# RWKV front and output projection with another ScalarE order, local attention in head pairs: a two-block network on one Trainium2 core

## The chip, the cores and the metric

One core of a Trainium2 chip runs the whole kernel. The metric is the device time of one launch in microseconds (us), taken as the median of several runs. TensorE (PE in the profile) multiplies; VectorE (DVE), ScalarE (ACT) and GpSimd (POOL) do the elementwise work; SyncE (SP) issues most DMAs.

## The reference

Input x has 256 tokens of 1024 channels. Four residual layers follow each other: RWKV-7 time mixing, local attention with sinks, a gated chunk mixer, forgetting attention; each has a feed-forward block behind it. The change touches the first two mixers:

```python
# RWKV-7: xr, xk, xv ... = x + (shifted x - x) * mu[i]
k = xk @ w_rkv[1]
w = -softplus(-(w_decay0 + tanh(xw @ w_decay1) @ w_decay2)) - 0.5
a = sigmoid(a0 + (xa @ a1) @ a2)
kk = heads(k * k_k); k = k * (1 + (a - 1) * k_a)
# S = S*decay + (S a) b^T + v k^T;  y = S r;  y = groupnorm(y)...
h = (y * g) @ w_o
x = x + rms_norm(h, g1);  x = x + conv_ffn(rms_norm(x, g2))
# local attention: 16 query heads on 4 key/value heads, window 128, 2 blocks
s = q k^T * 64**-0.5, masked;  m = max(max(s), sink)
p = exp(s - m);  denom = sum(p) + exp(sink - m)
o = (p / denom) @ v;  h = o @ w_o
```

All is float32. The kernel splits both operands of its large products into a part hi (rounded to the type fp32r that PE takes quickly) and the rest lo, and adds three products, hi*hi + lo*hi + hi*lo.

## The kernel before, in words

**Weights.** Weights of the large products arrive as units of 1 MB (`raw`, 128x2048). `split` makes hi by ScalarE casts (L120, four pieces of 512 columns) and lo by VectorE subtractions (L122). Six lo pieces, two each of units 57 to 59, go to GpSimd instead. A unit's `raw` buffer is refilled by a DMA on SP's queue when its pieces are done. `unit(ahead)` splits so many units ahead of the one handed out.

**Order.** Each engine runs its instructions in the order in which the program issues them; a scheduler sets that order from priorities, and `tc.issue_after(X)` keeps what is issued inside behind X. So a piece of ScalarE work that is ready can stand behind one that is not needed yet, and the reverse.

**RWKV front.** `pw` (L491) is the first low-rank product of decay and gate a; ScalarE turns it into `gw` (L492 tanh, L493 copy). `gw` feeds 32 matmuls `pz` (L512), in four groups m of eight; ScalarE takes the tanh of each (L517, tiles EE and av), VectorE makes the decay out of EE (L518) and runs scans (L530), whose exponentials ScalarE takes (L532, L533). Between them PE forms key blocks `pk` (`k_mm`, L564), of 8 contraction steps (16 records in the trace) each, on two PSUM buffers in turn. ScalarE reads a block by L570 and L571, VectorE by L573 (`kt`), which needs av; only then is its PSUM buffer free for the block after the next. `pn` (L584) are small norm products.

**RWKV output projection (wo).** `down` and `down_tail` multiply the group-normed y (`yT`, made by `gnT`, ScalarE L898 and VectorE L899) with units 16 to 19, tokens t=0 first, then t=1 into `dt`. `mid` runs `gnT(1, .)`. `done` squares the result on ScalarE (`jk_pn`, L175), builds the norm factor (L157 to L162, a short chain between ScalarE and VectorE) and adds the result to x. `nxt['go'](t)` squares the new x (`jk_n`), builds its factor, multiplies (`xn_n`, L227), transposes on PE (`pt_n`, L230) and splits it into X hi (ScalarE L240) and lo (VectorE L241); `nxt['front'](t)` multiplies the first block of the next layer (`F`).

**Local attention.** `swa` walks a list of tokens: `q` and `k` project, `s<n><hg>` forms scores of 128 tokens n and 8 heads hg (PE L1084, VectorE max L1087, ScalarE exponential L1096, VectorE scaling L1105), `p<n><hg>` transposes the probabilities (PE L1118), copies them out of PSUM (L1120) and multiplies with v (L1124, `pos`), `D` multiplies the first unit of the output projection `wo1`. A matmul of L1124 loads 64 columns of v and writes 64 of the 128 output partitions, the lower (e=0) or the upper half (e=1). In local attention the four matmuls of one PSUM buffer go by head; forgetting attention (`pof`) uses the same lines with heads of both halves in turn.

Of the kernel before, what the change touches and what calls it, by code (L numbers as in the profile page):

```python
# [55 lines left out]
def tile_net(ctx: ExitStack, tc: tile.TileContext, x_in, wst, lora1, lora2, cvec, cons, rows, sinks, w_s, foxf, out, dbg=None):  # L56
# [186 lines left out]
    def prep(key, norm=True, fold=False):  # L243
        o = {}

        def go(t):
            if t == 0:
                o['X'] = xhl(xp, f'X_{key}', bufs=1)
            rs = rms_of_x(t, key) if norm else None
            o[t] = rs  # L250
            to_T(t, rs, o['g'], key, *o['X'])
# [15 lines left out]
        o['go'] = go  # L267
        o['front'] = front
# [77 lines left out]
    def down_tail(acc, xs, us, nu, done, nxt):  # L346
        hls = [unit(ahead=len(us) + 2 - i) for i in range(len(us))]
        ga = {'kvg': 12, 'mx0': 12, 'ml1': 9, 'ml0': 9, 'mx1': 9, 'n12': 9, 'n02': 9}.get(nxt['key'] if nxt else '', 99)
        for t in range(2):
            if t and 'mid' in W:  # L350
                W.pop('mid')()
# [4 lines left out]
            for h in range(2):  # L356
# [67 lines left out]
    def rwkv(nxt):  # L424
        with tc.tile_pool(name='rw', bufs=1) as wp:
# [67 lines left out]
            A.copy(gw[64:128], pw[64:128, 0:T])  # L493
# [11 lines left out]
            Ei = EE[:, 32 * 65:].rearrange('p (q x) -> p q x', x=64)  # L505
            for m in range(4):
                pz = [psum(f'pz{m}{wa}', 'acc') for wa in range(2)]
                for f in range(2):
# [4 lines left out]
                for wa in range(2):
                    sg = Ei[:, 8 * m:8 * m + 8, :].rearrange('p c x -> p (c x)') if wa == 0 else av[:, 2 * m:2 * m + 2, :].rearrange('p j t -> p (j t)')
                    for f in range(2):
                        j = wa * 8 + 2 * m + f
                        A.activation(sg[:, f * T:(f + 1) * T], pz[wa][:, f * T:(f + 1) * T], AF.Tanh, bias=hb[:, j:j + 1], scale=0.5)  # L517
# [42 lines left out]
            def k_mm(u, f):  # L560
                w3 = kw[u].rearrange('p (k c) -> p k c', k=KD)
                pk = psum(f'pk{u}_{f}')[:, 0:T]
                for k in range(KD):
                    PE.matmul(pk, lhsT=w3[:, k, f * P:(f + 1) * P], rhs=XK[:, k, :], start=k == 0, stop=k == KD - 1)  # L564
# [5 lines left out]
                A.activation(s1[:, fs], pk, AF.Square, scale=cvc('k_k', j))  # L570
                A.activation(kkr[:, fs], pk, AF.Copy, scale=cvc('k_k', j))  # L571
# [310 lines left out]
            def gnT(t, hf):  # L882
# [15 lines left out]
                A.copy(YH[:, ks, tsl], p4)  # L898
                V.tensor_tensor(out=YL[:, ks, tsl], in0=p4, in1=YH[:, ks, tsl].bitcast(F32), op=ALU.subtract)  # L899
# [155 lines left out]
    def attend(ap, qT, kT, vv, oview, kidx, vidx, Lof, bias, sink, gate, nm, rsq=None):  # L1055
# [7 lines left out]
        def scores(n, hg):  # L1063
# [31 lines left out]
            for i in range(8):  # L1095
                A.activation(L[:, i, 0:nk], L[:, i, 0:nk], AF.Exp, bias=ng[:, i:i + 1], scale=1.0 if rsq is None else rsq[n], accum_out=dn[:, i:i + 1])  # L1096
            if sink is not None:
                sk = ap.tile([P, 8], F32, tag='sk', name=f'sk{nm}{n}{hg}', bufs=2)
                V.tensor_tensor(out=ej(sk), in0=sks, in1=ej(ng), op=ALU.add)
                A.activation(sk, sk, AF.Exp)  # L1100
                V.tensor_tensor(out=dn, in0=dn, in1=sk, op=ALU.add)
# [436 lines left out]
```

## Time and profile before

| what | value |
|---|---|
| median of 3 runs | 1349.07 us (1347.24 to 1349.47) |
| profiled execution, own time | 1347.06 us |
| its span, first to last instruction | 1345.4 us |
| PE busy | 1312.2 us, 98% |
| VectorE, ScalarE, GpSimd busy | 991.3 us (74%), 817.5 us (61%), 76.0 us (6%) |
| mean granted TensorE clock | 0.988 of full speed |
| HBM read | 222.32 MB, 166 GB/s over the span with what is written |

The share of busy time is a mean over the whole program; a PE that is 98% busy has 33 us of idle time in it, which stand at a few places. The list of waits names these places, and the timeline shows which engine worked in them.

### The profile page before, as it was taken

The numbers are of one execution on the slowest core, as the hardware profiler recorded it, in microseconds if no ns is written. First come the engines' busy times: TensorE is split into PE (matmuls) and PEld (weight loads), VectorE is DVE, ScalarE is ACT, GpSimd is POOL, SyncE is SP. The second block draws the span as 40 slices with busy tenths as digits, with TensorE's granted clock in tenths as the row PEclk, the third lists the DMA queues.
The fourth block names the chain that finished last, engine by engine and source line by source line (L and its number), as shares of the span: only waits on it lengthen the run. The fifth ranks groups of instructions, "written<-read, shape, count | busy, mean of one in ns | idle before, by whom it ended". The sixth has DMA issues, their size and how long they took to land.

```text
span 1345.4 us, 20651 instructions
## 1 busy us (share of the span) xinstructions
PE 1312.2 (98%) x7700; PEld 1108.6 (82%) x7700; DVE 991.3 (74%) x2200; ACT 817.5 (61%) x1803; POOL 76.0 (6%) x103
## 2 busy tenths in 40 slices
PE   7999997999999999999999999999999999999998
PEld 5785875888888878888888998888887888888887
DVE  5558676898888758998888976766667887676663
ACT  4505595776677856776777754655546667555551
POOL 4221400000000100000000000000000000000000
PEclk9899898999999999999999999999999999999999
DMA  9220232565544414655536553665543743265550
GB/s 358 71 86 1 96 104 108 199 247 194 202 168 142 154 66 157 235 212 204 192 130 235 188 187 124 234 218 189 188 168 118 280 150 133 98 243 191 189 188 32
DMA packets 34819, 224.70 MB, mean 167 GB/s; under 512 B 3712, under 2 KB 6048, under 8 KB 8736
## 3 DMA queue, kind: packets, MB, share of 16 engines
q1 hardware_dynamic: 32496, 215.18, 44.5%
q0 software_dynamic: 1472, 5.25, 1.1%
q10 hardware_dynamic: 752, 2.97, 0.6%
q8 instruction: 60, 0.98, 0.3%
q14 instruction: 39, 0.32, 0.1%
HBM read 222.32 MB, written 1.06 MB: 166 GB/s over the span
## 4 chain that ended last, share of the span: by engine, by line
PE 77%; DVE 3%; ACT 3%; DMA 1%; issue 1%; ACTq 0%
PE pu L299 10%; PE pm L299 7%; PE pu L297 6%; PE md L146 4%; PE md L147 4%; PE md L148 4%; PE pm L297 4%; PE fd L146 3%; PE fd L147 3%; PE fd L148 3%; PE pu L295 1%; PE gu L148 1%; PE gu L147 1%; PE gu L146 1%; PE go L146 1%; PE go L148 1%
## 5 line engine op out<-in xcount | busy, mean ns | idle before, releaser
L122 DVE TENSOR_TENSOR lo<-raw,hi 128x512 fp32r<-128x512 f32 x650 | 417.0, 687 | 81.0 <-ACT hi L120 79.6
L120 ACT CAST hi<-raw 128x512 fp32r<-128x512 f32 x656 | 365.1, 618 | 131.6 <-PE md L148 52.7
L299 PE MATMUL pu<-X_n_x,hi 128*128 128x512 f32 x560 | 142.1, 393 | 0.0
L299 PEld LDWEIGHTS pu<-X_n_x,hi 128*128 128x128 f32 x560 | 100.1, 189 | 17.5
L299 PE MATMUL pm<-X_ml_x,hi 128*128 128x512 f32 x392 | 99.7, 393 | 0.0
L297 PEld LDWEIGHTS pu<-X_n_x,lo 128*128 128x128 f32 x640 | 87.4, 190 | 6.2
L297 PE MATMUL pu<-X_n_x,lo 128*128 128x256 f32 x640 | 89.7, 283 | 0.0
L299 PEld LDWEIGHTS pm<-X_ml_x,hi 128*128 128x128 f32 x392 | 70.0, 189 | 12.2
L117 DVE SCALAR_TENSOR_TENSOR lo<-raw,cv,hi 128x256 fp32r<-128x256 f32 (+1 forms) x136 | 67.1, 561 | 14.0 <-ACT hi L116 13.8
L116 ACT ACTIVATE hi<-raw,cv 128x256 fp32r<-128x256 f32 (+1 forms) x136 | 65.7, 560 | 14.9 <-DMA raw<-in_wst 10.9
L304 ACT COPY r<-pm 128x256 f32<-128x256 f32 x56 | 20.9, 373 | 73.5 <-PE pm L299 73.5
L305 DVE TENSOR_TENSOR r<-pm,r 128x256 f32<-128x256 f32 x56 | 23.5, 425 | 56.9 <-ACT r L304 56.8
L297 PEld LDWEIGHTS pm<-X_ml_x,lo 128*128 128x128 f32 x448 | 61.2, 190 | 4.3
L297 PE MATMUL pm<-X_ml_x,lo 128*128 128x256 f32 x448 | 62.7, 282 | 0.0
L1012 ACT ACTIVATE ab<-zs,cv 128x256 f32<-128x256 f32 x80 | 47.8, 600 | 16.6 <-DVE zs L305 16.5
L147 PE MATMUL md<-lo,md0h 128*128 128x512 f32 x128 | 49.9, 390 | 0.0
L146 PE MATMUL md<-hi,md0h 128*128 128x512 f32 x128 | 49.8, 389 | 0.0
L146 PE MATMUL md<-hi,md1h 128*128 128x512 f32 x128 | 49.8, 389 | 0.0
L147 PE MATMUL md<-lo,md1h 128*128 128x512 f32 x128 | 49.8, 389 | 0.0
L148 PE MATMUL md<-hi,md0l 128*128 128x512 f32 x128 | 49.8, 389 | 0.0
L148 PE MATMUL md<-hi,md1l 128*128 128x512 f32 x128 | 49.8, 389 | 0.0
L1013 DVE SCALAR_TENSOR_TENSOR ab<-zs,cv,ab 128x255 f32<-128x255 f32 x80 | 38.6, 482 | 10.9 <-ACT ab L1012 9.3
(563 smaller groups left out, 3088.4 us busy)
## 6 DMA issues: line engine op xcount, KB each, us to landing
raw<-in_wst SPq DMA_DIRECT2D x188, 1024.0 KB, 4.9
kw<-in_wst SPq DMA_DIRECT2D x12, 1024.0 KB, 9.8
g_n<-in_rows POOLq DMA_DIRECT2D x6, 512.0 KB, 3.8
ncb<-cd ACTq DMA_DIRECT2D x2, 1024.0 KB, 5.8
l2g<-in_lora SPq DMA_DIRECT2D x1, 1024.0 KB, 14.6
g_ml<-in_rows POOLq DMA_DIRECT2D x2, 512.0 KB, 3.9
out<-x SPq DMA_DIRECT2D x4, 256.0 KB, 2.0
cs<-in_cons SPq DMA_DIRECT2D x1, 513.0 KB, 9.2
```

Of the source, the lines that this page charges most:

```text
L116: A.activation(hi[:, q:q + w], r[:, q:q + w], AF.Copy, scale=g[:, j:j + 1])
L117: V.scalar_tensor_tensor(out=lo[:, q:q + w], in0=r[:, q:q + w], scalar=g[:, j:j + 1], in1=hi[:, q:q + w].bitcast(F32), op0=ALU.mult, op1=A ...
L120: A.copy(hi[:, q:q + SPL], r[:, q:q + SPL])
L122: pe_.tensor_tensor(out=lo[:, q:q + SPL], in0=r[:, q:q + SPL], in1=hi[:, q:q + SPL].bitcast(F32), op=ALU.subtract)
L146: W['mm'].append(PE.matmul(o, lhsT=lh, rhs=rh, start=start, stop=False))
L147: PE.matmul(o, lhsT=lh, rhs=rl, start=False, stop=False)
L148: PE.matmul(o, lhsT=ll, rhs=rh, start=False, stop=stop)
L297: W['mm'].append(PE.matmul(pt[:, 0:T], lhsT=l3[:, k, fs], rhs=X2[:, 0, k, :], start=False, stop=False))
L299: PE.matmul(pt, lhsT=h3[:, k, fs], rhs=X2[:, :, k, :], start=False, stop=k == KD - 1)
L305: V.tensor_tensor(out=out, in0=pt[:, 0:T], in1=out, op=ALU.add)
L1012: A.activation(ab[:, s, :], z, AF.Identity, bias=cw(3, fi), scale=cw(2, fi))
L1013: V.scalar_tensor_tensor(out=ab[:, s, 1:T], in0=z[:, 0:T - 1], scalar=cw(1, fi), in1=ab[:, s, 1:T], op0=ALU.mult, op1=ALU.add)
```

## The change

It does the following:

- Front: ScalarE takes `gw` (L492, L493) ahead of the six reads of `pk` that stood before it; the reads of the fourth and later key blocks stand behind the last tanh issued (`th`); PE forms the fourth key block (2u+f = 3) behind the second group of `pz`.
- wo: `mid` returns the subtractions of `gnT(1, .)`, and units 16 and 17's last splits are issued behind them, so `yT` goes ahead of the casts; a new `rms(0)` issues the squares of x's first tokens as soon as they are there.
- Local attention: scores, exponentials, scaling, transposes and the products with v go in pairs of heads, one of each half (0, 4, 1, 5, ...); the token order puts the first tokens' last heads (`s01`) ahead and their softmax in a step of its own (`e01`); the first unit of wo1 runs t=1 before t=0. In forgetting attention, exponential and scaling go in the order of pairs too.
- GpSimd's six lo pieces go to VectorE.

```diff
             else:
                 for q in range(0, 2048, SPL):
                     A.copy(hi[:, q:q + SPL], r[:, q:q + SPL])
-                    pe_ = G if {57: 12, 58: 12, 59: 12}.get(i, 0) >> q // SPL & 1 else V
-                    pe_.tensor_tensor(out=lo[:, q:q + SPL], in0=r[:, q:q + SPL], in1=hi[:, q:q + SPL].bitcast(F32), op=ALU.subtract)
+                    V.tensor_tensor(out=lo[:, q:q + SPL], in0=r[:, q:q + SPL], in1=hi[:, q:q + SPL].bitcast(F32), op=ALU.subtract)
...
+        def rms(t):
+            if norm:
+                o['rs0'] = rms_of_x(t, key)
...
-            rs = rms_of_x(t, key) if norm else None
+            rs = o.pop('rs0', None) or rms_of_x(t, key) if norm else None
...
     def down_tail(acc, xs, us, nu, done, nxt):
-        hls = [unit(ahead=len(us) + 2 - i) for i in range(len(us))]
+        hls = [unit(ahead=len(us) + 2 * ('mid' not in W) - i) for i in range(len(us))]
...
             if t and 'mid' in W:
-                W.pop('mid')()
+                for an in W.pop('mid')():
+                    late.enter_context(tc.issue_after(an.ins))
+                split(W['u'] + 2)
+                late.close()
...
+            if nxt is not None and t == 0 and ga < 99:
+                with tc.high_priority():
+                    nxt['rms'](0)
...
-            A.copy(gw[64:128], pw[64:128, 0:T])
+            gwi = A.copy(gw[64:128], pw[64:128, 0:T])
...
-                for k in range(KD):
-                    PE.matmul(pk, lhsT=w3[:, k, f * P:(f + 1) * P], rhs=XK[:, k, :], start=k == 0, stop=k == KD - 1)
+                with tc.issue_after(pzm[1].ins) if 2 * u + f == 3 else nullcontext():
+                    for k in range(KD):
+                        PE.matmul(pk, lhsT=w3[:, k, f * P:(f + 1) * P], rhs=XK[:, k, :], start=k == 0, stop=k == KD - 1)
...
-                A.activation(s1[:, fs], pk, AF.Square, scale=cvc('k_k', j))
-                A.activation(kkr[:, fs], pk, AF.Copy, scale=cvc('k_k', j))
+                with tc.issue_after((gwi if j < 3 else th).ins):
+                    A.activation(s1[:, fs], pk, AF.Square, scale=cvc('k_k', j))
+                    A.activation(kkr[:, fs], pk, AF.Copy, scale=cvc('k_k', j))
...
                 with tc.issue_after(W['mm'][-5].ins):
                     for hf in range(2):
-                        gnT(1, hf)
+                        an = gnT(1, hf)
+                return an
...
-                ss_ = [i0 + i if KZ else (i0 + i) // 2 + 4 * (i % 2) for i in range(per)]
+                ss_ = [(i0 + i) // 2 + 4 * (i % 2) for i in range(per)]
...
-                for i, b in [(i, b) for i in range(per) for b in range(n + 1)] if KZ else [(i, b) for b in range(n + 1) for i in range(per)]:
+                for i, b in [(i, b) for b in range(n + 1) for i in range(per)]:
...
-            for tk in 'q0 k0 k1 q1 s10 q2 s00 q3 s11 p10 p00 s01 D p11 p01'.replace('/', ' ').split():
+            TOK = 'q0 k0 k1 q1 s10 q2 s00 q3 s01 p10 e01 p00 s11 D p01 p11'.split()
...
+                elif tk[0] == 'e':
+                    with tc.issue_after(st['ox', 1, 0].ins):
+                        st.pop(('e', int(tk[1]), int(tk[2])))()
...
-                    for t in range(2):
+                    for t in (1, 0):
```

**ScalarE in the RWKV front, before** (EE and av rows of L517 are the tanh of `pz`, L570 and L571 the reads of `pk`):

```order
L570 ACTIVATE AR<-pk_0_347,cv 128x256
...
L571 ACTIVATE kkr_384<-pk_0_375,cv 128x256
L492 ACTIVATE gw<-pw 64x256
L493 COPY gw<-pw 64x256
L570 ACTIVATE AR<-pk_1_389,cv 128x256
L571 ACTIVATE kkr_384<-pk_1_389,cv 128x256
L517 ACTIVATE EE<-pz_240,hb 128x256 x2
L517 ACTIVATE av<-pz_241,hb 128x256 x2
L517 ACTIVATE EE<-pz_252,hb 128x256 x2
L517 ACTIVATE av<-pz_253,hb 128x256 x2
L532 ACTIVATE EE<-AR 128x8x64
```

The same place now:

```order
L503 ACTIVATE gw<-pw 64x256
L504 COPY gw<-pw 64x256
L584 ACTIVATE AR<-pk_0_347,cv 128x256
...
L585 ACTIVATE kkr_384<-pk_0_375,cv 128x256
L529 ACTIVATE EE<-pz_240,hb 128x256 x2
L529 ACTIVATE av<-pz_241,hb 128x256 x2
L529 ACTIVATE EE<-pz_252,hb 128x256 x2
L529 ACTIVATE av<-pz_253,hb 128x256 x2
L544 ACTIVATE EE<-AR 128x8x64
L545 ACTIVATE EE<-AR 128x512
L544 ACTIVATE EE<-AR 128x8x64
L545 ACTIVATE EE<-AR 128x512
L529 ACTIVATE EE<-pz_264,hb 128x256 x2
```

`gw` moved ahead of the six reads, the fourth block's reads (`pk_1_389`) moved away, and four exponentials now stand ahead of the third group's tanh, where one stood.

**ScalarE in the wo tail, before** (`dt` is the second tokens' result, `x_66` the residual of the first tokens):

```order
L890 ACTIVATE ya_1900<-pyt_1891,cv 128x128 x3
L120 CAST hi_1779<-raw_1742 128x512 x4
L120 CAST hi_1789<-raw_1753 128x512 x4
L898 CAST yT<-ya_1900 128x4x128
L175 ACTIVATE jk_pn_1935,ss_pn_1936<-dt_1909 128x512
L175 ACTIVATE jk_n_1967,ss_n_1968<-x_66 128x512
L175 ACTIVATE jk_n_1972,ss_n_1973<-x_66 128x512
L157 ACTIVATE rs_n_1977<-ss_n_1973,bb_n_1970 128x1
L175 ACTIVATE jk_pn_2028,ss_pn_2029<-dt_1910 128x512
```

The same place now:

```order
L904 ACTIVATE ya_1898<-pyt_1889,cv 128x128 x3
L174 ACTIVATE jk_n_1851,ss_n_1852<-x_66 128x512
L174 ACTIVATE jk_n_1856,ss_n_1857<-x_66 128x512
L912 CAST yT<-ya_1898 128x4x128
L156 ACTIVATE rs_n_1861<-ss_n_1857,bb_n_1854 128x1
L120 CAST hi_1907<-raw_1742 128x512 x4
L120 CAST hi_1917<-raw_1753 128x512 x2
L174 ACTIVATE jk_pn_1953,ss_pn_1954<-dt_1927 128x512
L120 CAST hi_1917<-raw_1753 128x512 x2
L174 ACTIVATE jk_pn_2028,ss_pn_2029<-dt_1928 128x512
```

Two squares and the `yT` cast stand ahead of the eight casts, where `yT` stood behind all eight.

**VectorE at the end of wo1, before** (n120 is the norm of the first tokens for the next feed-forward block, pn111 the norm of wo1's result for the second tokens):

```order
L162 SCALAR_TENSOR_TENSOR rsq_n120_4937<-rv_n120_4938,ry_n120_4940 128x1
L227 SCALAR_TENSOR_TENSOR xn_n1200_4947<-x0_66,rsq_n120_4937,g_n12_4787 128x512
L158 TENSOR_SCALAR rv_pn111_4996<-ss_pn1111_4991,bb_pn111_4906 128x1
L159 RECIPROCAL ry_pn111_4998<-rs_pn111_4997 128x1
L227 SCALAR_TENSOR_TENSOR xn_n1201_4956<-x0_66,rsq_n120_4937,g_n12_4787 128x512
```

The same place now:

```order
L158 RECIPROCAL ry_n120_4896<-rs_n120_4895 128x1
L157 TENSOR_SCALAR rv_pn111_4996<-ss_pn1111_4991,bb_pn111_4924 128x1
L159 TENSOR_TENSOR rv_n120_4894<-rv_n120_4894,ry_n120_4896 128x1
L158 RECIPROCAL ry_pn111_4998<-rs_pn111_4997 128x1
L160 TENSOR_TENSOR rv_n120_4894<-rv_n120_4894,ry_n120_4896 128x1
L159 TENSOR_TENSOR rv_pn111_4996<-rv_pn111_4996,ry_pn111_4998 128x1
L161 SCALAR_TENSOR_TENSOR rsq_n120_4893<-rv_n120_4894,ry_n120_4896 128x1
L160 TENSOR_TENSOR rv_pn111_4996<-rv_pn111_4996,ry_pn111_4998 128x1
L226 SCALAR_TENSOR_TENSOR xn_n1200_4947<-x0_66,rsq_n120_4893,g_n12_4787 128x512
```

Two rows of pn111, whose inputs `ss_pn1111` and `rs_pn111` come from the last matmul of wo1, stand ahead of `xn_n1200` now; before, they stood behind it.

## Rows read from the trace of the kernel before

**Rows 1.** Page, span and busy time of each engine.

```profile
span 1345.4 us, 20651 instructions
PE 1312.2 (98%) x7700; PEld 1108.6 (82%) x7700; DVE 991.3 (74%) x2200; ACT 817.5 (61%) x1803; POOL 76.0 (6%) x103
```

**Rows 2.** List of PE's waits: line waited for, us in total, times, longest us.

```profile
PE dt L146 <- ACT yT L898: 3.5, 1, 3.5
PE pz L512 <- ACT gw L492: 2.7, 1, 2.7
PE wo L148 <- DVE ox_x L1130: 2.0, 1, 2.0
```

**Rows 3.** Timeline of ScalarE, front: start, duration, instruction, [idle before <- releaser].

```profile
29.57 0.47 ACT L570 ACTIVATE AR<-pk,cv 128x256 f32<-128x256 f32 x1 [12.30 <-issue]
...
31.73 0.38 ACT L492 ACTIVATE gw<-pw 64x256 f32<-64x256 f32 x1
...
38.96 0.84 ACT L517 ACTIVATE EE<-pz,hb 128x256 f32<-128x256 f32 x2
```

**Rows 4.** Timeline of PE, front.

```profile
15.51 10.52 PE L564 MATMUL pk<-XRK,kw 128*128 128x256 f32 x48
...
32.16 0.70 PE L512 MATMUL pz<-gw,l2a 64*128 64x256 f32 x2 [2.68 <-ACT gw L492]
32.79 5.41 PE L564 MATMUL pk<-XRK,kw 128*128 128x256 f32 x16
...
47.68 5.12 PE L564 MATMUL pk<-XRK,kw 128*128 128x256 f32 x16 [1.26 <-DVE kt L573]
```

**Rows 5.** Timeline of VectorE, front.

```profile
42.45 1.56 DVE L530 TENSOR_TENSOR_SCAN AR<-cs,EE 128x256 f32<-128x256 f32 x2
...
47.21 0.74 DVE L573 TENSOR_TENSOR kt<-kt,pk 128x256 f32<-128x256 f32 x2
```

**Rows 6.** Windows: busy us of PE, PEld, DVE, ACT, POOL; granted clock, DMA share, GB/s.

```profile
44.00:46.00 2.00, 2.00 (x10) 1.68 (x10) 1.02 (x5) 0.73 (x2) 0.62 (x1) 0.50 0.00 0
216.00:218.00 2.00, 2.00 (x6) 1.51 (x6) 0.11 (x1) 0.00 (x0) 0.00 (x0) 0.55 1.05 426
```

**Rows 7.** Timeline of ScalarE, wo tail.

```profile
209.95 4.26 ACT L120 CAST hi<-raw 128x512 fp32r<-128x512 f32 x8 [4.26 <-PE dt L148]
214.11 0.61 ACT L898 CAST yT<-ya 128x512 fp32r<-128x512 f32 x1
...
221.77 0.29 ACT L157 ACTIVATE rs_n<-ss_n,bb_n 128x1 f32<-128x1 f32 x1
```

**Rows 8.** Timeline of VectorE, wo tail.

```profile
207.65 0.68 DVE L893 TENSOR_TENSOR ya<-ya,gt 128x512 f32<-128x512 f32 x1
```

**Rows 9.** Timeline of PE, wo tail.

```profile
214.78 0.79 PE L146 MATMUL dt<-hl,yT 128*128 128x512 f32 x1 [3.46 <-ACT yT L898]
...
223.68 1.78 PE L230 MATMUL pt_n<-cs,xn_n 128*128 128x128 f32 x8 [1.63 <-DVE xn_n L227]
...
232.27 1.38 PE L230 MATMUL pt_n<-cs,xn_n 128*128 128x128 f32 x8
```

**Rows 10.** Timeline of PE, local attention (pos) and forgetting attention (pof).

```profile
460.81 3.33 PE L1124 MATMUL pos<-PTs,vv 128*64 128x128 f32 x32
...
1137.81 1.09 PE L1124 MATMUL pof<-PTf,vvf 128*64 128x128 f32 x16
```

**Rows 11.** Timeline of VectorE, scaling of probabilities in local attention.

```profile
451.33 2.19 DVE L1105 TENSOR_SCALAR Ls<-Ls,rds 128x256 f32<-128x256 f32 x8
...
470.18 4.25 DVE L1105 TENSOR_SCALAR Ls<-Ls,rds 128x256 f32<-128x256 f32 x8
```

**Rows 12.** Timelines of ScalarE and VectorE at the end of wo1.

```profile
503.33 0.60 ACT L175 ACTIVATE jk_pn<-wo 128x512 f32<-128x512 f32 x1 [0.85 <-PE wo L148]
...
503.71 0.75 DVE L227 SCALAR_TENSOR_TENSOR xn_n<-x,rsq_n,g_n 128x512 f32<-128x512 f32 x1
```

**Rows 13.** Window in the second feed-forward block, columns as in rows 6.

```profile
537.60:571.20 33.60, 33.60 (x180) 29.01 (x179) 32.17 (x67) 26.35 (x58) 0.00 (x0) 1.00 0.66 229
```

More of the change, by code (lines that the diff above doesn't have):

```diff
@@ L267, in prep @@
         o['go'] = go
+        o['rms'] = rms
         o['front'] = front
@@ L505, in rwkv @@
             Ei = EE[:, 32 * 65:].rearrange('p (q x) -> p q x', x=64)
+            pzm = {}
             for m in range(4):
@@ L897, in gnT @@
                 YH, YL = Y
-                A.copy(YH[:, ks, tsl], p4)
-                V.tensor_tensor(out=YL[:, ks, tsl], in0=p4, in1=YH[:, ks, tsl].bitcast(F32), op=ALU.subtract)
+                yh = A.copy(YH[:, ks, tsl], p4)
+                return yh, V.tensor_tensor(out=YL[:, ks, tsl], in0=p4, in1=YH[:, ks, tsl].bitcast(F32), op=ALU.subtract)
             def two(f, c):
@@ L1080, in scores @@
             for i0 in range(0, 8 * KZ, per):
+                ss_ = [(i0 + i) // 2 + 4 * (i % 2) for i in range(per)]
                 pl = psum(f'pl{nm}{n}{hg}{i0}')
                 for i in range(per):
-                    h = hd(hg, i0 + i)
+                    h = hd(hg, ss_[i])
                     PE.matmul(pl[:, i * nk:(i + 1) * nk], lhsT=qT[:, h // 2, n * P:(n + 1) * P], rhs=kT[:, kidx(h), h % 2, 0:nk], start=True, stop=True)
                 for i in range(per):
-                    h = hd(hg, i0 + i)
-                    V.tensor_tensor_reduce(out=L[:, i0 + i, 0:nk], in0=pl[:, i * nk:(i + 1) * nk], in1=bias(n, hg, i0 + i), scale=1.0, scalar=-3e+38, op0=ALU.add, op1=ALU.max, accum_out=mx[:, i0 + i:i0 + i + 1])
+                    s_ = ss_[i]
+                    V.tensor_tensor_reduce(out=L[:, s_, 0:nk], in0=pl[:, i * nk:(i + 1) * nk], in1=bias(n, hg, s_), scale=1.0, scalar=-3e+38, op0=ALU.add, op1=ALU.max, accum_out=mx[:, s_:s_ + 1])
             if rsq is not None:
@@ L1094, in scores, with soft @@
             V.tensor_scalar_mul(ng, mx, -1.0)
[L1095 to L1101, printed above, removed]
-            rd = ap.tile([P, 8], F32, tag='rd', name=f'rd{nm}{n}{hg}', bufs=2)
-            V.reciprocal(out=rd, in_=dn)
-            for i in range(8):
-                V.tensor_scalar_mul(L[:, i, 0:nk], L[:, i, 0:nk], rd[:, i:i + 1])
-            st[n, hg] = L
+            def soft():
+                for i in [i // 2 + 4 * (i % 2) for i in range(8)]:
+                    A.activation(L[:, i, 0:nk], L[:, i, 0:nk], AF.Exp, bias=ng[:, i:i + 1], scale=1.0 if rsq is None else rsq[n], accum_out=dn[:, i:i + 1])
+                if sink is not None:
+                    sk = ap.tile([P, 8], F32, tag='sk', name=f'sk{nm}{n}{hg}', bufs=2)
+                    V.tensor_tensor(out=ej(sk), in0=sks, in1=ej(ng), op=ALU.add)
+                    A.activation(sk, sk, AF.Exp)
+                    V.tensor_tensor(out=dn, in0=dn, in1=sk, op=ALU.add)
+                rd = ap.tile([P, 8], F32, tag='rd', name=f'rd{nm}{n}{hg}', bufs=2)
+                V.reciprocal(out=rd, in_=dn)
+                for i in [i // 2 + 4 * (i % 2) for i in range(8)]:
+                    V.tensor_scalar_mul(L[:, i, 0:nk], L[:, i, 0:nk], rd[:, i:i + 1])
+                st[n, hg] = L
+            if defer:
+                st['e', n, hg] = soft
+            else:
+                soft()
         def pv(n, hg, tag='acc'):
@@ L1114, in pv @@
                 pt = psum(f'ptr{nm}{n}{hg}{i0}')
-                ss_ = [i0 + i if KZ else (i0 + i) // 2 + 4 * (i % 2) for i in range(per)]
+                ss_ = [(i0 + i) // 2 + 4 * (i % 2) for i in range(per)]
                 for i in range(per):
@@ L1128, in pv @@
             if gate is None:
-                (A.copy, V.tensor_copy)[0](oh, p4)
+                st['ox', n, hg] = A.copy(oh, p4)
                 V.tensor_tensor(out=ol, in0=p4, in1=oh.bitcast(F32), op=ALU.subtract)
@@ L1134, in pv @@
                 split_act(oh, ol, o)
-        return (scores, pv)
+        return (scores, pv, st)
     def swa(pre, nxt):
@@ L1187, in oview @@
                 return (OX[0][:, ks, tsl], OX[1][:, ks, tsl])
[L1188 removed]
+            scores, pv, st = attend(ap, qT, kT, vv, oview, lambda h: h // 4, lambda h: h // 4, lambda n, hg: ap.tile([P, 8, 256], F32, tag='L', name=f'Ls{n}{hg}', bufs=3), lambda n, hg, s: band if n == 1 else band[:, 128:256], sk, None, 's', rss)
             acc, nd = (None, 0)
[L1190 removed]
+            TOK = 'q0 k0 k1 q1 s10 q2 s00 q3 s01 p10 e01 p00 s11 D p01 p11'.split()
+            for tk in TOK:
                 if tk[0] == 'k':
```

12 lines of the change are left out of this document (6 added, 6 removed).

## The prediction

> **What bounds the kernel now.** The page comes first: PE is busy for 1312.2 of 1345.4 us [rows 1], so nothing is to be had from the other engines' work as such, only from the 33 us in which PE waits, and from places where PE's own work runs long. The list of PE's waits says where they are [rows 2]. The reader is to see that three of the longest lie at places which the change reorders: `dt` behind the `yT` cast, 3.5 us; `pz` behind `gw`, 2.7; `wo` behind `ox_x`, 2.0. The third view, the timelines of the engines named, shows whether such a wait is needed or only queued for [rows 3 to 5, 7 to 9, 11, 12]. The fourth, the windows, shows that a wait costs more than itself: the granted clock is 0.50 at 44 to 46 us and 0.55 at 216 to 218, 1.2 instead of 2.4 GHz, each time after PE stood idle [rows 6]. A key block that takes 10.52/3 = 3.5 us among the first three takes 5.41 behind such a wait [rows 4].
>
> The sum is made against the profiled execution, 1347.06 us (span 1345.4), which is 2.0 us below the median of 1349.07; I subtract the same difference from both. A difference under 0.2%, 2.7 us, could not be told from none.
>
> **Front.** Before, ScalarE reads three key blocks from 29.57 to 31.73, 2.16 us, and only then makes `gw` from the finished `pw` [rows 3]; PE waits 2.68 us, does two `pz`, then spends 5.41 us on a key block, and the first tanh starts at 38.96 [rows 3, 4]. Now `gw` starts at 29.57, `pz` follows near 30.0, ScalarE reads the key blocks until 32.5 and goes on to the tanh of groups 0 and 1: 6.4 us earlier. That is the most there can be. The end of this stretch is set by another chain: the fifth key block waits at 47.68 for `kt` [rows 4, 5]. I follow it: eight tanh at 0.36 us (the step of the six equal-sized reads, 2.16/6) until 35.4; on VectorE one 0.4 us step and a pair of scans, 1.56 us, per group [rows 5], ending near 37.6; the exponentials of group 1 until 38.7. They now stand ahead of group 2's tanh, which before ran without them; so group 2 starts at 38.7 where its `pz` has long been there. Its step and scans end near 41.7, then `vn` 0.2 and `kt` 0.7 (half of 47.21's pair after L572): 42.7 to 43.2. PE's key block starts near 43.4 instead of 47.68. **Gain 4.3 us.** Ends: 3.0, if the scheduler's order puts one more pair of scans (1.56) ahead of `kt`; 6.0, if `kt` is as much earlier as the tanh less one pair of exponentials. PE then idles before `kt` as before, so I leave the half-rate block of 5.12 us as it is.
>
> **wo tail.** `ya`, which `yT` is cast from, is ready at 207.65 + 0.68 = 208.33 [rows 8], but the cast stands behind eight casts of weights, 4.26 us, until 214.11; PE waits 3.46 us [rows 7, 9]. Now two squares of x stand there from about 207.05 to 208.65, then `yT` to 209.26, before PE's first half is out of work at 214.78 - 3.46 = 211.3. The wait goes, and with it the half rate behind it, some 3 us of which [rows 6] show two at 0.55: 1.4 us. Against 223.68 - 1.63 = 222.05 `dt` would end 3.46 + 1.4 + 0.2 (a pipeline that needn't fill anew) earlier, near 216.9. The factor `rs_n`, at 221.77 before [rows 7], comes before 210, so `xn_n` is no longer late (1.63 us, [rows 9]), but the splits fall due then: lo of the first X waits on VectorE, about 0.75 us. The second tokens' transposes, at 232.27 [rows 9], need the whole chain square, factor, add, square, factor, multiply behind `dt`; I get 226.3 for them, with PE idle 1.45 us ahead of them where it was not before, and the clock may fall once (0.7 of a chance at 1.4 us is part of the lower end). **Gain 5.3 us**, ends 3.5 and 6.5 (3.46 + 1.63 + 1.4). Moved past: units 16 and 17 are split later, so the buffer of unit 19 is refilled later, landing near 226 by my count against a need near 228; SP's order is unchanged.
>
> **Attention.** The 96 records of L1124 take about 10 us in all; 32 in a row take 3.33, 0.104 each; in the forgetting attention, where neighbours write different halves, 16 take 1.09, 0.068 each [rows 10]. With the spacing inside a run, 0.099 against 0.055, that is 0.044 x 96 = 4.2 us. A second part: the scaling of eight probabilities takes 4.25 us beside GpSimd's lo pieces and 2.19 without [rows 11]; the 2.0 us wait for `ox_x` [rows 2] stands directly behind it, since L1130 is queued there. The six pieces cost VectorE six times about 0.7 (an equal-sized subtraction, [rows 8]), 4.1 us, hidden behind wo1's matmuls, which leave VectorE waiting for their sums. Following the new token order I find wo1 ending at 497.0 instead of 503.3: 4.2 from the pairs and 2.1 from waits. Of this some is given back. Before, `xn_n` starts at 503.71, 0.4 us behind the last `wo` [rows 12]. Now two steps for the last sum stand ahead of it on VectorE, and they wait for the end of wo1, a square (0.7), a factor (0.3) and six chain steps at 0.2: PE idles about 3.7 us instead of some 1.3, 2.4 us lost, and after such an idle of 3.46 us [rows 9] the clock fell; that costs up to 1.5 us here, 1.0 with its chance. Net **gain 3.2 us** (6.3 - 2.4 + 0.4 from nearer transposes - 1.0), ends 1.0 and 5.2.
>
> On the pairs a rule speaks against the change. The row shows one thing only, that the 16 take 1.09 us there [rows 10]. The Trainium skill, page "TensorEngine Tiling (Array Packing)", section "PSUM Bottleneck", states that tiling speeds up TensorE but not the evacuation of PSUM, so that the copy may become the bottleneck. By that, the twelve copies of `PTs` would set the pace, the 4.2 us would be lost and the sum would be 8.6. No row of this case decides it; it is one of the rivals below, as a mechanism of this kernel.
>
> **Small edits.** Forgetting attention's new order of exponentials and scaling has the same count of instructions; its waits are elsewhere. 0, ends 0 and 0.5. Should the cover go (its exponentials lie beside PE's `g` products), the price is one exponential, about 0.5 us.
>
> **Sum:** 4.3 + 5.3 + 3.2 = 12.8 us. 1347.06 becomes 1334.3, and the median 1349.07 becomes **1336.3**. The three pairs of ends added give 7.5 and 17.7, or 1341.6 to 1331.4.
>
> **The rivals.**
> A. As worked out: 1336.3. For it: each wait named is a queue order and not missing work.
> B. The half rate goes too: without the long idles PE keeps its clock, `pk` at 3.5 instead of 5.12 us, and all upper ends hold: 17.7, 1331.4. For it: each stretch at half rate that was shown stands behind an idle that this change shortens. Against it: I still count idles of 1.5 and 3.7.
> C. Attention gives nothing: the copies `PTs` pace the pairs, or neighbours of two halves don't overlap here as they do in [rows 10]; the 4.2 us go, and the late `xn_n` still costs: 3.2 - 4.2 = -1.0, so 4.3 + 5.3 - 1.0 = 8.6, 1340.5. For it: each `pos` group waits on a transposed copy, and the groups in wo1 are only eight long.
> D. Slower. In the feed-forward blocks VectorE works 32.17 of 33.6 us [rows 13], 1.43 us free in a window. If it is the last to end there, PE's gains in front of it are given back at its next weights, and the six moved pieces, 4.1 us, come on top: 1349.07 + 4.1 = 1353.2. It decides when VectorE's lead in hi/lo pieces is less than what PE gains, about 10 us. Against it: PE is 33.60 of 33.6 busy there, so VectorE keeps up.
> E. The front doesn't do what it says, since `kt` and not `gw` ends it, and the late transposes take the wo gain: 2 us, 1347.
>
> **How the numbers follow.** A 0.55, B 0.14, C 0.20, D 0.05, E 0.06. Range 1330.5 to 1342: A with its ends, B and C; it leaves out D, E and 0.07 of A, B and C. Faster by over 0.2%: A, B, C and a third of E, 0.91. Slower: D, 0.05. Same: the rest, 0.04.
>
> **What would show it.** `pz` starts near 30.0 and the fifth key block near 43.4 in PE's timeline; the wait of `dt` for `yT` is gone and the second tokens' `pt_n` starts some 6 us earlier relative to the first `dt`; L1124's runs take 0.07 us a record and L1105's last eight 2.2 us; `pt_n` in front of the second feed-forward block waits 3 to 4 us. It is wrong if these hold and the span does not fall (VectorE took it back, D), or if `dt` waits for a weight unit instead.

## The result and the profile after

The changed kernel takes 1330.21 us (median of 4 runs, 1329.78 to 1332.21) against 1348.15 us of the kernel before on the same chips, ratio 0.9874 with an interval of 0.986 to 0.9887: 17.0 us less by the ratio, 17.9 by the two medians. Forecast were 12.8 us less, 1336.3, and a range of 1330.5 to 1342. The sign and most of the mechanisms held; 1330.21 lies 0.3 us under the lower end, while the ratio applied to the 1349.07 of the forecast gives 1332.1, inside it.

The profiled execution took 1332.21 us, 14.85 us less than the one before (1347.06). It is the slowest of its four, while the one before lies 1.1 us under its median, so two to three of the 17 to 18 us lie outside these two profiles and are not placed below. The page of after, span and busy time, answers to [rows 1]:

```profile
span 1330.5 us, 20649 instructions
PE 1303.5 (98%) x7700; PEld 1102.7 (83%) x7700; DVE 990.2 (74%) x2206; ACT 815.6 (61%) x1803; POOL 68.2 (5%) x97
```

PE's busy time fell by 8.7 us, so more than half of the gain is not idle time: it is PE work that ran at full clock, or as pairs (3.8 us of it in the products with v, 10.7 to 6.9). The list of PE's waits of after shows the rest, beside [rows 2]:

```profile
PE pt_n L229 <- DVE xn_n L226: 3.9, 2, 3.1
PE pn L598 <- ACT EE L529: 2.0, 1, 2.0
...
PE pk L577 <- DVE kt L587: 1.3, 1, 1.3
...
PE pz L524 <- ACT gw L503: 0.5, 1, 0.5
```

The waits for `yT` (3.5) and for `ox_x` (2.0) are gone, that for `gw` fell from 2.7 to 0.5. Two waits have grown: 2.0 for EE in the front, and 3.1 for `xn_n` in front of the second feed-forward block. In the list of before these are:

```profile
PE pt_n L230 <- DVE rv_pn L158: 1.3, 1, 1.3
...
PE pn L584 <- ACT EE L517: 0.8, 1, 0.8
```

**Front.** The timelines of after, PE's, ScalarE's and VectorE's, answer to [rows 3 to 5]:

```profile
29.65 2.38 PE L524 MATMUL pz<-gw,l2a 64*128 64x256 f32 x16 [0.47 <-ACT gw L503]
31.97 3.72 PE L577 MATMUL pk<-XRK,kw 128*128 128x256 f32 x16
...
39.21 1.50 PE L598 MATMUL pn<-cs,AR 128*128 128x2 f32 x8 [2.03 <-ACT EE L529]
...
43.12 5.36 PE L577 MATMUL pk<-XRK,kw 128*128 128x256 f32 x16 [1.25 <-DVE kt L587]
```

```profile
32.17 0.88 ACT L529 ACTIVATE EE<-pz,hb 128x256 f32<-128x256 f32 x2
```

```profile
39.19 0.43 DVE L530 TENSOR_SCALAR EE<-EE 128x512 f32<-128x512 f32 x1 [1.94 <-ACT EE L529]
...
42.00 0.73 DVE L586 TENSOR_SCALAR kt<-av,cv,oka 128x256 f32<-128x256 f32 x2 [0.48 <-issue]
42.65 0.74 DVE L587 TENSOR_TENSOR kt<-kt,pk 128x256 f32<-128x256 f32 x2
```

The first tanh starts at 32.17, 6.8 us earlier. The fourth key block now takes 3.72 instead of 5.41 us: PE no longer stands idle for 2.68 us before it, and the clock stays at 1.00. The fifth starts at 43.12 behind `kt` and runs at half rate (1.2 GHz) again. It is 4.56 us earlier than at 47.68. The windows, before inside the fourth block, after inside the fifth:

```profile
34.00:36.00 2.00, 2.00 (x6) 1.61 (x5) 0.00 (x0) 0.00 (x0) 0.00 (x0) 0.50 0.00 0
```

```profile
44.00:46.00 2.00, 2.00 (x6) 1.55 (x6) 2.00 (x5) 1.23 (x3) 2.00 (x3) 0.50 0.00 0
```

**wo tail.** PE's timeline of after, beside [rows 9], and a window behind the last wait shown:

```profile
212.38 1.03 PE L229 MATMUL pt_n<-cs,xn_n 128*128 128x128 f32 x8
213.86 0.50 PE L145 MATMUL F_n<-hi,X_n_x 128*128 128x512 f32 x1 [0.44 <-ACT X_n_x L239]
...
220.97 1.38 PE L229 MATMUL pt_n<-cs,xn_n 128*128 128x128 f32 x8 [0.80 <-DVE xn_n L226]
```

```profile
222.00:224.00 2.00, 2.00 (x12) 1.53 (x11) 1.54 (x3) 1.43 (x4) 0.41 (x1) 1.00 0.40 133
```

The first tokens' transposes follow `dt` without a wait, 11.3 us earlier than at 223.68; the second tokens', at 220.97, are 11.3 us earlier too. The first `dt` comes at 199.53, 4.4 us earlier, so this stretch alone gave 6.9. The clock stays at 1.00 from 204 to 226 us here; before, it fell behind the wait for `yT` [rows 6].

**Attention and the second feed-forward block.** PE, the first run of L1146 (L1124 before), the last `wo`, and what follows it; then the windows there:

```profile
447.99 2.00 PE L1146 MATMUL pos<-PTs,vv 128*64 128x128 f32 x32
...
484.47 0.40 PE L147 MATMUL wo<-hi,ox_x 128*128 128x512 f32 x1
487.97 1.94 PE L229 MATMUL pt_n<-cs,xn_n 128*128 128x128 f32 x8 [3.10 <-DVE xn_n L226]
```

```profile
488.00:490.00 2.00, 2.00 (x9) 1.78 (x10) 1.46 (x4) 0.64 (x2) 0.00 (x0) 0.50 0.00 0
490.00:492.00 2.00, 2.00 (x5) 1.53 (x6) 2.00 (x4) 1.41 (x4) 0.53 (x1) 0.50 0.27 98
```

32 records take 2.00 us instead of 3.33 [rows 10]. The last `wo` starts 18.4 us earlier than before (502.90), 7.1 us more than the 11.3 with which the stretch began; then the 3.1 us wait and the half rate behind it take 3 us back. One window in the feed-forward block answers to [rows 13]: PE is busy in all of it, VectorE for 31.59.

```profile
537.60:571.20 33.60, 33.60 (x179) 28.99 (x178) 31.59 (x66) 26.74 (x59) 0.00 (x0) 1.00 0.61 208
```

Placed by stretch, the profile's 14.85 us are: front 4.4, wo tail 6.9, attention 7.1, in front of the second feed-forward block -3.0, everything behind that -0.6.

### The profile page after: what moved, and what is told of

The parts are those of the page before. It is cut to its first block, busy times and chain, and to the rows that moved or that the text cites. A ratio compares the mean times of both kernels' runs of the same rounds, so it can differ in the third digit from the quotient of the medians.

```text
span 1330.5 us, 20649 instructions
## 1 busy us (share of the span) xinstructions
PE 1303.5 (98%) x7700; PEld 1102.7 (83%) x7700; DVE 990.2 (74%) x2206; ACT 815.6 (61%) x1803; POOL 68.2 (5%) x97
## 4 chain that ended last, share of the span: by engine, by line
PE 77%; ACT 4%; DVE 3%; DMA 1%; issue 1%; ACTq 0%
PE pu L303 10%; PE pm L303 7%; PE pu L301 6%; PE md L147 4%; PE md L145 4%; PE md L146 4%; PE pm L301 4%; PE fd L147 3%; PE fd L146 3%; PE fd L145 3%; PE pu L299 1%; PE gu L147 1%; PE gu L145 1%; PE gu L146 1%; DMA raw<-in_wst 1%; PE go L145 1%
```

## The experiments

**The three parts alone.** Each kernel is the one before with the edits of one part of the change as the diff shows them (the attention part with GpSimd's pieces and forgetting attention's order).

> Only the edits of the RWKV front (gw ahead of the key blocks' reads, later reads behind the last tanh, fourth key block behind the second group of pz); the rest is the kernel before. Theory 1 (the parts are independent, each worth its own stretch): the fifth key block starts 4.6 us earlier and the whole kernel is 4.4 us faster, ratio 0.9967. Rival (the front's gain is lost or doubled further on, since VectorE or a weight transfer ends the next stretch): the first dt starts less than 3 us or more than 6 us earlier, ratio above 0.998 or below 0.9955.

> Only the edits of the wo tail (splits behind the transposes, squares of x early; the latter hold in front of the other feed-forward blocks with a norm too); the rest is the kernel before. Theory 1: PE's 3.5 us wait for yT goes, and with it the two stretches at half clock behind it; the second tokens' transposes start 6.9 us earlier, the whole is 6.9 us faster, ratio 0.9949. Rival (the sum of my prediction: 0.8 us wait for lo and a fall of the clock stay): 5.3 us, ratio 0.9961.

> Only the edits of the attention (pairs of heads, token order, deferred softmax, wo1's first unit, GpSimd's pieces to VectorE, forgetting attention's order); front and wo tail as before. Without the early squares xn stands ahead of the last sum's chain again as in the kernel before. Theory 1 (6.3 us up to the end of wo1, 3.0 of them given back by the early squares' order in front of the second feed-forward block): wo1 ends 6.3 us earlier, and the whole is 5 to 6 us faster, ratio 0.996. Rival (the give-back comes from the attention edits themselves): wo1 ends 6.3 us earlier but the whole is only 3.3 us faster, ratio 0.9975.

Measured, as ratio to before: front 0.9977 (0.9965 to 0.9989), wo tail 0.9949 (0.9932 to 0.9966), attention 0.9956 (0.9938 to 0.9973). That is 3.1, 6.9 and 5.9 us; the sum, 15.9, is near the whole, 17.0. That fits parts that are independent, as theory 1 has it; each interval is 1.6 to 2.4 us wide to either side, so an exchange of a few us between them is not excluded.

In the wo tail both signs of theory 1 hold: the wait is gone, and counted from the first `dt` the second tokens' transposes come 7.0 us earlier. The time alone, 0.9949, does not exclude the rival's 0.9961.

The front's 3.1 us lies under 4.4, though the interval reaches 4.7 and the fifth key block of that kernel starts 4.1 us earlier. Its profiled execution shows a loss further on: it is 4.8 us ahead of before at the end of the wo tail, 2.2 at the end of wo1 and 0.6 at the end. In local attention `pls` waits 1.5 us for `qT` there, where before shows 0.5, and the clock falls, where before is at 1.00 from 472 to 476:

```profile
472.00:474.00 2.00, 2.00 (x7) 1.52 (x6) 0.90 (x4) 1.23 (x5) 0.00 (x0) 0.50 0.22 41
```

This execution took 1346.49 us, 2.1 above the median of ten. Whether part of the front's gain is lost there as a rule stays open.

The attention part brought a miss. Theory 1 put the give-back down to the early squares, which that kernel does not have. The wait is there all the same (PE's timeline of it):

```profile
498.69 1.36 PE L229 MATMUL pt_n<-cs,xn_n 128*128 128x128 f32 x8 [3.13 <-DVE rsq_pn L161]
502.02 0.50 PE L147 MATMUL F_n<-hi,X_n_x 128*128 128x512 f32 x1 [1.30 <-DVE bb_n L178]
```

So the give-back comes with the attention edits themselves, as the rival said. The time lies with theory 1 all the same, and the rival's 0.9975 just outside the interval: the clock did not fall behind that wait (last section), and of the 6.4 us by which its profile is shorter, 7.1 came between the first scores and the last `wo` (65.5 us before, 58.4 here and in the changed kernel), 2.3 were given back up to the last F, and 1.6 lie at other places.

**Pairs.** The changed kernel with plain head order (one of five places shown; the others are the same exchange in scores, exponential, scaling and transposes):

```diff
-                for i, b in [(i, b) for b in range(n + 1) for i in range(per)]:
+                for i, b in [(i, b) for i in range(per) for b in range(n + 1)] if KZ else [(i, b) for b in range(n + 1) for i in range(per)]:
```

> The changed kernel with heads in their plain order again: scores, exponentials, scaling, transposes and the products with v of local attention by head, as before; the token order and all else as changed (forgetting attention's exponentials and scaling are by head again too). Theory 1 (pairs of heads overlap on PE): records of L1124 take 0.10 us in a run instead of 0.066, the kernel is 3 to 4.2 us slower than the changed one, ratio to before 0.990. Rival (token order and the moved lo pieces made the gain): records may run slow, but the time stays with the changed kernel's, ratio 0.9874, since other engines end the stretch.

Measured: ratio 0.9906 (0.9884 to 0.9928) where the changed kernel has 0.9874 and, run once more, 0.9883: 3.1 to 4.3 us slower, with intervals that overlap, so the trace has to decide. PE's timeline of it, the run of 32:

```profile
448.00 3.33 PE L1146 MATMUL pos<-PTs,vv 128*64 128x128 f32 x32
```

The last `wo` of it comes 4.5 us later than in the changed kernel; counted from the first scores, 5.7 us, of which 3.9 are the matmuls of L1146 themselves (10.8 us busy against 6.9) and 1.3 waits of `pls` and `pos`. Theory 1 holds: it is the neighbours in two halves, not the token order, that make 0.104 into 0.063 us a record.

**Early squares.** The changed kernel without `rms`:

```diff
-            if nxt is not None and t == 0 and ga < 99:
-                with tc.high_priority():
-                    nxt['rms'](0)
```

> The changed kernel without the early squares: the norm of x's first tokens is formed where it was before, ahead of the last matmuls of the layer (this holds for the wo tail and in front of the second and fourth feed-forward-like blocks with a norm). Theory 1 (the early squares give the wo tail 1.6 us, as the first tokens' transposes need no wait, and little elsewhere): 1 to 2.5 us slower than the changed kernel, ratio to before 0.989; in the wo tail a wait of 1 to 2 us for xn behind dt comes back. Rival (the yT cast gives it all, and the early squares cost in front of the second feed-forward block): the same time or up to 2 us faster.

Measured: ratio 0.9935 (0.9917 to 0.9953); against the changed kernel's 0.9874 and 0.9883 that is 7 to 8 us slower, 5.0 by the profiles. Both theories are off, theory 1 by its size. PE's timeline of it in the wo tail:

```profile
215.21 1.39 PE L229 MATMUL pt_n<-cs,xn_n 128*128 128x128 f32 x8 [2.58 <-DVE xn_n L226]
218.57 0.80 PE L147 MATMUL F_n<-hi,X_n_x 128*128 128x512 f32 x1 [1.22 <-DVE bb_n L178]
```

With the `yT` cast ahead alone, the wait for `yT` turns into one of 2.6 us for `xn_n` and one of 1.2 for X, and half rate behind them (0.50 from 218 to 222 us). From the last `dt` to the last F it takes 20.0 us, against 15.8 in the changed kernel and 17.6 before: 4.3 us more than with the squares early. From the first `dt` on, the cast alone gives 4.2 of the 6.9 us, 1.6 of them because this execution has no stretch at half rate behind the first `dt`, where both others have one. The squares alone were not run. The time holds more than this stretch: in front of the second feed-forward block, too, this kernel needs 1.3 us more from the last `wo` to the last F.

**GpSimd's pieces.** The changed kernel with the six pieces on GpSimd, the line of the diff undone.

> The changed kernel with GpSimd's six lo pieces back on GpSimd. Theory 1 (GpSimd beside VectorE doubles the scaling of eight probabilities, 2.19 to 4.25 us, and the wait for ox_x behind it returns): one run of L1105's eight takes over 3 us, the end of wo1 is up to 2 us later, ratio to before 0.9885. Rival (in the new token order the scaling is no longer awaited): the scaling is slower but the time is the changed kernel's within 0.1%.

Measured: ratio 0.9882 (0.9865 to 0.9898), not to be told from the changed kernel. VectorE's timeline shows that the slowing is there, on another group of eight than before (1.65 us in the changed kernel):

```profile
455.38 3.81 DVE L1124 TENSOR_SCALAR Ls<-Ls,rds 128x128 f32<-128x128 f32 x8
```

Two waits of `pos` for its copies come with it:

```profile
PE pos L1147 <- ACT PTs L1143: 1.8, 1, 1.8
...
PE pos L1147 <- DVE PTs L1143: 1.5, 1, 1.5
```

From the first scores to the last `wo` PE takes 62.0 us, against 58.4 in the changed kernel: 3.6 us more, of which these waits are 3.3. In the time it could not be seen; this one execution was faster than the changed kernel's first in the wo tail, where the two do not differ. The 2.0 us that I gave these pieces are neither confirmed nor excluded by the time. Of the rival its time holds, but not its reason, since `pos` does wait.

**The wait in front of the second feed-forward block.** Three versions: the square root's table loaded earlier; the last sum's chain behind `xn`; both. The first is one line, the second an order on VectorE:

```diff
+            pre_sqrt(OX[0][0:1, KD - 1, T - 1:T].bitcast(F32))
             g1 = grow('n11')
```

```diff
         A.activation(s, ss, AF.Sqrt, bias=b, scale=4.0 * scale)
-        V.tensor_scalar(out=v, in0=ss, scalar1=-4.0 * scale, scalar2=b, op0=ALU.mult, op1=ALU.subtract)
...
+        with tc.issue_after(W['xni'].ins) if nm == 'pn111' else nullcontext():
+            V.tensor_scalar(out=v, in0=ss, scalar1=-4.0 * scale, scalar2=b, op0=ALU.mult, op1=ALU.subtract)
...
```

> The changed kernel with one more ScalarE instruction: a square root of one element behind the last output cast of local attention, so that the square root's table is loaded (1.28 us) while ScalarE waits for wo1, and not in the first norm of wo1's result. Theory 1 (the 3.1 us wait in front of the second feed-forward block is set by the first tokens' norm chain, whose first step waits for the table): the first tokens' transposes start 1.2 us earlier, the wait is 1.9 us, the time 1 to 3 us less, ratio to before 0.986. Rival (the wait is set by the last sum's chain that stands ahead of xn on VectorE): xn_n1200 stands behind the first step for the last sum still, which waits for the end of wo1, so the transposes move by less than 0.5 us.

> The changed kernel with VectorE's chain for the last sum of wo1 (second tokens) put behind the first tokens' xn in front of the second feed-forward block, as the order was before; the table is loaded where the changed kernel loads it. Theory 1 (the first tokens' own chain, late by the table, ends the wait): transposes 0.3 us earlier, wait 2.8 us, time the same within 0.1%. Rival (the interleaved rows cause the give-back of 2.4 us that my prediction named): wait about 1.3 us, time 2 to 4 us less.

> Both: the table loaded early, and the last sum's chain behind the first tokens' xn. Theory 1: wait near 1.5 us, transposes 1.5 us earlier than in the changed kernel; no stretch at half clock in front of the second feed-forward block; time 1.5 to 3.5 us less than the changed kernel's, ratio to before 0.985. Rival (the second tokens, whose norm is now later, become the wait): the gain of the first tokens is lost at the second tokens' transposes, time unchanged.

Measured: table 0.9857 (0.9829 to 0.9886), chain behind `xn` 0.9881 (0.9862 to 0.9901), both 0.9848 (0.9825 to 0.9872); the changed kernel, beside them on the same chip, 0.9883 (0.9864 to 0.9902). PE's timelines at the transposes, in this order:

```profile
489.58 1.35 PE L229 MATMUL pt_n<-cs,xn_n 128*128 128x128 f32 x8 [2.09 <-DVE ry_pn L158]
```

```profile
486.96 1.29 PE L232 MATMUL pt_n<-cs,xn_n 128*128 128x128 f32 x8 [2.98 <-DVE xn_n L227]
```

```profile
483.20 1.29 PE L232 MATMUL pt_n<-cs,xn_n 128*128 128x128 f32 x8 [2.10 <-DVE xn_n L227]
```

The wait goes from 3.10 to 2.09 with the table, to 2.98 with the order, to 2.10 with both. So the first tokens' own chain sets it, with the table's load as 1.0 us of it, and not the interleaved rows that I had named; the 1.5 us expected of both is a miss, since the order adds nothing to the table. The medians of table and both lie 2 and 5 us under the changed kernel's, but the intervals overlap: not settled by themselves. The positions say more. The starts of the last `wo` and of the last F behind it, in us:

| kernel | last `wo` | last F | between |
|---|---|---|---|
| before | 502.90 | 518.72 | 15.8 |
| changed | 484.47 | 503.26 | 18.8 |
| changed, run again | 484.33 | 502.52 | 18.2 |
| chain behind `xn` | 483.58 | 501.16 | 17.6 |
| table | 487.09 | 503.62 | 16.5 |
| both | 480.70 | 497.40 | 16.7 |

With the table early, the stretch takes 1 to 2 us less.

**`kt` early.** The changed kernel, in which VectorE stood idle for 1.94 us before group 2's step and did `kt` only behind it:

```diff
+                if j < 2:
+                    tc.add_manual_dep(sg2.ins, kti.ins.name, mybir.DependencyInfo(mybir.DependencyClass.NoSync, mybir.DependencyReason.DATA), reason='kt')
...
-                pin(K(0, 0), K(0, 1), K(1, 0), K(1, 1), N_(0), K(2, 0), N_(1), K(2, 1), K(3, 0), N_(2), K(3, 1))
+                pin(K(0, 0), K(0, 1), K(1, 0), K(1, 1), K(2, 0), N_(0), N_(1), K(2, 1), K(3, 0), N_(2), K(3, 1))
```

> The changed kernel with VectorE's kt of the first two key blocks ordered ahead of the decay step of group 2, and PE's fifth key block ahead of the first norm product. Theory 1 (VectorE's order, kt behind the scans of group 2, sets the fifth key block at 43.1 us; nothing else is needed for it): the fifth key block starts at 37 to 39 us, PE's 2.0 and 1.25 us waits go, time 2 to 5 us less than the changed kernel's, ratio to before 0.985. Rival (the exponentials and norm chains behind are the bound, so the wait moves to the next norm product or transposes): fifth block early, but the time within 1 us of the changed kernel's.

> kt early, the square root's table early and the last sum's chain behind xn, all three. Theory 1 (the three stretches add): 3.5 to 8 us less than the changed kernel, ratio to before 0.983. Rival (front gain lost before the recurrence): as the version with the latter two, ratio 0.985.

Measured: `kt` early 0.9843 (0.9828 to 0.9858), and with table and chain 0.9831 (0.9816 to 0.9845), 1324.75 us, the fastest of all; both lie below the changed kernel by intervals that do not touch its own; the two are not told from each other. PE's and VectorE's timelines of the first:

```profile
39.36 3.72 PE L579 MATMUL pk<-XRK,kw 128*128 128x256 f32 x16 [1.25 <-DVE kt L589]
```

```profile
38.24 0.74 DVE L588 TENSOR_SCALAR kt<-av,cv,oka 128x256 f32<-128x256 f32 x2 [0.50 <-issue]
38.90 0.74 DVE L589 TENSOR_TENSOR kt<-kt,pk 128x256 f32<-128x256 f32 x2
```

The fifth block starts at 39.36 and takes 3.72 instead of 5.36 us. The time of `kt` early is 4.2 to 5.4 us less by the ratios, where theory 1 had 2 to 5. Not all of it came as expected: the block starts later than at 37 to 39 us, and the wait of 1.25 us for `kt` is still there. That VectorE's order alone did it is not shown, since the edit also puts PE's fifth key block ahead of the first norm product. In the changed kernel PE waits 2.03 us for EE before that product and only 1.25 for `kt` behind it; so VectorE's order alone could bring the block forward by those 1.25 us, to 41.9 by my estimate, and the rest up to 39.36 needs PE's order too. No run separates the two.

**The changed kernel again.**

> The changed kernel once more, for a second profile of it: the first profiled execution took 1332.21 us at a mean clock of 0.990, the three others near 1330.1 at 0.993. Theory 1 (the difference is one stretch at half clock, which comes in some executions and not in others): in an execution near 1330 one of the stretches at half clock that the first profile shows (near 42, 145, 202, 490, 1099 us) is missing, and the instructions behind it stand 1 to 2.5 us earlier. Rival (another engine or a transfer is late in the first execution): the same stretches, and the difference lies elsewhere.

Measured: 1331.14 us, ratio 0.9883 (0.9864 to 0.9902). The execution profiled took 1331.92, hardly less than the first, so its time does not settle theory 1. Its trace does: one stretch at half rate of the first profile, near 202 us, is missing. The same window, first profile, then this one:

```profile
202.00:204.00 2.00, 2.00 (x7) 1.63 (x6) 1.99 (x5) 1.27 (x4) 0.00 (x0) 0.63 0.01 4
```

```profile
202.00:204.00 2.00, 2.00 (x10) 1.64 (x9) 1.93 (x6) 0.58 (x3) 0.00 (x0) 1.00 0.01 4
```

From the first to the last `dt` it takes 11.1 us instead of 12.6, and counted from the first `pz` the last `dt` is 2.1 us earlier. The total hides it, since this execution starts later, the first `pz` at 31.34 instead of 29.65. So half rate differs between executions of one program. In front of the second feed-forward block, behind the same 3.10 us wait, the window from 488 to 490 is at 0.86 here, where the first profile had 0.50.

```profile
487.82 1.29 PE L229 MATMUL pt_n<-cs,xn_n 128*128 128x128 f32 x8 [3.10 <-DVE xn_n L226]
```

```profile
488.00:490.00 2.00, 1.95 (x11) 1.07 (x9) 1.92 (x5) 1.17 (x2) 0.52 (x1) 0.86 0.00 0
490.00:492.00 2.00, 2.00 (x6) 1.61 (x6) 1.78 (x4) 1.45 (x4) 0.00 (x1) 0.50 0.63 209
```

## Why the prediction was right, point by point

**Front: 4.3 forecast, 4.56 at the fifth key block, 4.4 at the first `dt`.** The chain was the right one: `gw` at 29.2, the tanh 6.8 us earlier, exponentials ahead of group 2, `kt` at 42.65. The gain is less than the 6.4 us that I gave as ScalarE's lead because the order of VectorE and PE ends the stretch, and `kt` early shows that this was order and not work.

**wo tail: 5.3 forecast, 6.9 measured.** The mis-sized term is the second tokens' transposes. My 226.3 for them is 6.0 us under 232.27; counted from the first `dt` they came 6.9 earlier. I counted 1.45 us of idle PE there, and PE waits 0.80. The step from 6.0 down to the 5.3 that I booked is not worked out in the prediction; it may stand for the 0.7 of a chance that the clock falls, and the clock stays at 1.00 up to 226 us. I also gave the early squares only the 1.63 us wait that they remove. Without them the changed kernel loses 4.3 us in this stretch: once `yT` is early, the norm of the first tokens is what is late next, and half rate follows it. The wait that the trace of before shows is what remains behind another wait, and no price of the edit that ends it.

**Attention: 6.3 up to the end of wo1 forecast, 7.1 measured.** The pairs give 3.1 to 4.3 us by the times of the run without them and 5.7 up to the end of wo1 by its trace, 4.2 forecast; L1124's busy time falls by 3.8, from 10.7 to 6.9 us. The waits gave more than the 2.1 forecast: before, PE waits 2.0 and 1.1 us for `ox_x` and 0.5 for `qT`, now 0.8 in all, 2.8 less. I had counted the first of these alone. What GpSimd's pieces cost is open, between nothing by the times and 3.6 us by one trace.

On the rule of the Trainium skill ("TensorEngine Tiling (Array Packing)", section "PSUM Bottleneck"): here the copies did not become the bound. PE's waits for `PTs` in the changed kernel sum up to 0.2 us, and the loss of 4.2 us that I drew from the rule did not come. The Trainium skill says so in that section for a fourfold speed-up of TensorE. The pairs give a factor of 1.7 (3.33 against 2.00 us), so no run here tests the rule where it is stated. The copies are not far from binding: with GpSimd's pieces back, the waits for `PTs` are 3.3 us. On the same page of the Trainium skill, the section "Key Properties" states that different tiles can run in parallel; that agrees with 2.00 against 3.33 us for the same 32 records.

**Give-back: 3.0 forecast (2.4 + 1.0 - 0.4), 3.0 measured.** The size was right by luck, since the cause was not. (My net gain of 3.2 is 0.1 under 6.3 - 3.0.) I named the two steps for the last sum ahead of `xn_n`. The run that puts them behind it leaves the wait at 2.98 of 3.10 us; the run with the table early takes 1.0 us off. The load of the table, 1.28 us, stands on ScalarE in the first norm of wo1's result, but it stood there before the change as well. ScalarE before, then ScalarE and VectorE of after; the first line of each is the square of the first tokens' last sum:

```profile
495.95 0.60 ACT L175 ACTIVATE jk_pn<-wo 128x512 f32<-128x512 f32 x1 [0.76 <-PE wo L148]
...
496.66 1.28 ACT L157 ACT_TABLE_LOAD   x1
```

```profile
479.39 0.60 ACT L174 ACTIVATE jk_pn<-wo 128x512 f32<-128x512 f32 x1 [0.77 <-PE wo L147]
...
480.09 1.28 ACT L156 ACT_TABLE_LOAD   x1
```

```profile
487.07 1.41 DVE L226 SCALAR_TENSOR_TENSOR xn_n<-x,rsq_n,g_n 128x512 f32<-128x512 f32 x2
```

From this square to `xn_n` the chain takes 7.8 us before (to 503.71 [rows 12]) and 7.7 now: it has not grown. What has shrunk is PE's work beside it. Before, wo1 ends 7.3 us behind the start of the square, with 32 records of `wo` left; now 5.5 us, with 24. The difference of 1.9 us is the growth of the wait, from 1.3 to 3.1. The attention part alone has the same 5.5 us. So the new order of wo1's matmuls, which leaves fewer of the second tokens' products for the end, takes away the cover. Which of its edits does it, t=1 ahead in the first unit or the token order, no run separates.

**Rivals.** B comes nearest in time, 17.7 us, but not by its mechanism: the front's fifth block still runs at half rate in the changed kernel, and so does, in its first profile, the stretch behind the 3.1 us wait. C is excluded by the pairs, D by PE's 33.60 of 33.6 us in the feed-forward block, E by the front alone. Of the signs that I named, `pz` at 29.65, the missing wait for `yT`, 0.063 us a record and the wait of 3.1 us came as said.

## What to carry to other kernels

A wait in a list is priced by what ends it and by what is late next: trace the second chain to its end before giving an edit its gain, and take two edits that clear one after the other as one. If ScalarE, VectorE and PE run in program order, look for the engine that idles while a ready instruction stands behind one that is not; here `kt` could run at 38.24 instead of 42.00 us. A chain can become late without growing, when the work that covered it moves elsewhere. Matmuls that use half the columns go in pairs of both halves (0.063 instead of 0.104 us a record here).

## What the hardware showed that I had not expected

The clock's fall is not a fixed price of an idle time. Behind a wait of 3.1 us in front of the second feed-forward block, PE ran at 0.50 from 488 to 492 in the first profile of the changed kernel; in the second profile, with the same wait, at 0.86 and 0.50; in the attention part alone, with 3.13 us, at 1.00 in the windows from 498 to 504:

```profile
498.00:500.00 2.00, 1.21 (x9) 0.85 (x9) 1.92 (x5) 0.59 (x1) 0.00 (x0) 1.00 0.00 0
500.00:502.00 2.00, 0.71 (x3) 0.28 (x2) 2.00 (x6) 1.82 (x4) 0.53 (x1) 1.00 0.17 63
```

So a term for half rate can only be a chance. A second source of scatter is the start: in the eleven profiles of kernels with the new front, the first `pz` starts between 29.10 and 32.14 us, and a position is best counted from a point shortly ahead of its stretch. The times of one program scatter accordingly, by 2.4 us in the four runs of the changed kernel, by 6.1 in thirteen runs of the one before, and by 9.2 in the four with the early table.
